# A row-sum kernel: the second load moved from ahead of the opening barriers to behind them

## The chip, the cores and the metric

The kernel runs on one core of a Trainium2 chip. The metric is the device time of one execution, in microseconds (us). Before the change the median of three runs is 160.56 us (160.53 to 160.62).

## The reference

```python
def setup_inputs():
    batch, seq, dim = 32, 512, 1024
    return {"x": np.random.randn(batch, seq, dim).astype(np.float32)}

def reference(x):
    return np.sum(x, axis=-1).astype(np.float32)
```

16384 rows of 1024 float32 values are summed to one value each: 67.1 MB are read, 64 KB are written, and there is one addition for each value read.

## The kernel before, in words

The rows are spread over the 128 partitions of the on-chip memory, 128 rows to each. `BLOCKS = (113, 15)` cuts a partition's 128 rows into two runs, each contiguous in memory. They are loaded in pieces, in this order (the list `loads`, L92 to L100):

- the *lead*: row 0 of every partition, into a buffer of its own (512 KB in all, 4 KB for each partition);
- seven blocks into three rotating buffers `xt0` to `xt2`: six blocks of 16 rows (8 MB, 64 KB for each partition) and one of 15 rows. Each buffer has a semaphore, `slot0` to `slot2`;
- three pieces of 9, 4 and 2 rows (`CUTS`), and the last row in two pieces of 576 and 448 values (`CUT`).

All loads are issued from SyncE's queue (SP, L139). The lead and the first three blocks wait for nothing, since their buffers are empty. Every later load into a rotating buffer first waits until VectorE (DVE) has reduced the block that lay there (L138).

DVE reduces a block with one `tensor_reduce` over 16 rows (L57), after waiting for the block's semaphore. It does the lead first (L105, L106), then the blocks in order. ScalarE (ACT) takes a share of the rows of the last blocks and pieces (L68), and the last row is summed by DVE in two halves (L75). SP stores the results: the two early stores at L145 when most sums are there, the last 16 sums of each partition at L148.

What sets the order around the change is the code at L164 to L183, which edits the finished program. A program of this kind opens with three barriers at which all five engines meet (they carry the lines L197 and L158 in the profile). At each, an engine drains its own queue, reports to GpSimd (POOL), and waits until GpSimd has collected all reports and releases it. The kernel's own instructions stand in a block behind these barriers. The code takes the first `EARLY` load issues out of that block and puts them in front of SP's first drain, ahead of the first barrier. It may do so because these loads wait for nothing. With `EARLY = 2` the lead and block 0 (16 rows, buffer `xt0`, semaphore `slot0`) are issued there; blocks 1 and 2 follow behind the third barrier.

Of the kernel before, what the change touches and what calls it, by code (L numbers as in the profile page):

```python
# [12 lines left out]
ACT_ROWS = 7  # L13
CUT = 576
CUTS = (0, 9, 13, 15)
EARLY = 2


def row_sums(nc, x: bass.AP, out: bass.AP):
# [136 lines left out]
def kernel(tc: tile.TileContext, x: bass.AP, out: bass.AP):  # L156
# [17 lines left out]
    code = list(body.instructions)  # L174
    loads = [i for i in code if i.engine == sp and i.opcode == "DMACopy"][:EARLY]
    for load in loads:
# [36 lines left out]
```

## Time and profile before

One execution was profiled. Its span runs from the first to the last instruction, here from the issue of the lead on SP.

| quantity | value |
|---|---|
| median of three runs | 160.56 us |
| the profiled execution | 160.63 us |
| its span | 159.3 us |
| DVE busy | 121.6 us |
| ACT busy | 17.2 us |
| read from HBM | 67.11 MB, 422 GB/s over the span |
| lead: issue to landing | 3.4 us |
| block 0: issue to landing | 22.3 us |
| the two early stores, the last store: issue to landing | 1.6, 1.4 us |

In the profile's rows, L139 is line 139 of the kernel; "xt<-in_x_dram" names the destination and the source; "x3" counts instructions. A timeline row has the start in us, the length in us, the engine and line, the operation, and in brackets how long the engine sat idle before it and what ended the wait. SPq, POOLq, ACTq and so on are the instruction queues of the engines: issuing, draining and waiting, not computing. A load's packets are the pieces that the 16 DMA engines move one after the other; in this kernel a packet is one partition's share of a load, so a load has 128 of them, 8 for each DMA engine. "Landing" is the time at which all of a load's data and its semaphore counts have arrived.

### The profile page before, as it was taken

The numbers are of one execution on the slowest core, as the hardware profiler recorded it, in microseconds if no ns is written. First come the engines' busy times: TensorE is split into PE (matmuls) and PEld (weight loads), VectorE is DVE, ScalarE is ACT, GpSimd is POOL, SyncE is SP. The second block draws the span as 40 slices with busy tenths as digits, with TensorE's granted clock in tenths as the row PEclk, the third lists the DMA queues.
The fourth block names the chain that finished last, engine by engine and source line by source line (L and its number), as shares of the span: only waits on it lengthen the run. The fifth ranks groups of instructions, "written<-read, shape, count | busy, mean of one in ns | idle before, by whom it ended". The sixth has DMA issues, their size and how long they took to land.

```text
span 159.3 us, 108 instructions
## 1 busy us (share of the span) xinstructions
DVE 121.6 (76%) x17; ACT 17.2 (11%) x31; POOL 0.2 (0%) x4
## 2 busy tenths in 40 slices
DVE  1100029999499995999869996899959999797685
ACT  3000000000000000000000000000000000394694
POOL 0000000000000000000000000000000000000000
DMA  9969979989699699699699797996996999699994
GB/s 395 527 263 527 477 313 527 411 378 527 280 510 527 263 527 527 263 527 510 280 527 444 346 527 313 477 527 263 527 510 278 463 494 494 296 444 444 395 400 143
DMA packets 2304, 67.18 MB, mean 422 GB/s; under 512 B 640, under 2 KB 768, under 8 KB 1024
## 3 DMA queue, kind: packets, MB, share of 16 engines
q1 hardware_dynamic: 2304, 67.18, 98.1%
HBM read 67.11 MB, written 0.07 MB: 422 GB/s over the span
## 4 chain that ended last, share of the span: by engine, by line
DMA 75%; DVE 22%; SPq 1%; issue 0%
DMA xt<-in_x_dram 51%; DMA tail<-in_x_dram 24%; DVE res L57 22%; SPq L139 1%; DVE pairs L75 0%; DVE res L75 0%
## 5 line engine op out<-in xcount | busy, mean ns | idle before, releaser
L57 DVE TENSOR_REDUCE res<-xt 128x16 f32<-128x16384 f32 (+3 forms) x9 | 118.7, 13191 | 32.5 <-DMA xt<-in_x_dram 32.5
L68 ACT ACTIVATE xt<-xt 128x1024 f32<-128x1024 f32 x15 | 15.6, 1043 | 138.1 <-DMA xt<-in_x_dram 138.1
L68 ACT ACTIVATION_READ_ACCUMULATOR xt<-xt 128x1 f32 x15 | 2.8, 187 | 0.0
L57 DVE TENSOR_REDUCE res<-lead 128x1 f32<-128x1024 f32 x1 | 1.2, 1220 | 1.4 <-DMA lead<-in_x_dram 1.4
L103 DVE MEMSET tail<- 128x1 f32 x1 | 0.1, 59 | 2.0 <-PEq L158 2.0
L68 ACT ACT_TABLE_LOAD x1 | 1.3, 1283 | 1.9 <-PEq L158 1.9
L75 DVE CUSTOM_DVE_ANT_0 pairs<-tail 128x288 f32<-128x288 f32 (+1 forms) x2 | 0.9, 426 | 0.1
L75 DVE CUSTOM_DVE_ANT_0 pairs<-xt 128x512 f32<-128x512 f32 x1 | 0.7, 692 | 0.2 <-DMA xt<-in_x_dram 0.2
L75 DVE DVE_READ_ACCUMULATOR2_ANT res<- 128x1 f32 x2 | 0.2, 82 | 0.0
L197 POOL MEMSET const-uint8-127<- 128x1 uint8 x1 | 0.1, 103 | 0.0
L197 POOL MEMSET const-bfloat16-1.0<- 128x1 bf16 x1 | 0.1, 102 | 0.0
L197 POOL MEMSET const-float32-0.0<- 128x1 f32 x1 | 0.1, 98 | 0.2 <-issue 0.2
L197 POOL MEMSET const-float32-1.0<- 128x1 f32 x1 | 0.1, 98 | 0.0
L75 DVE DVE_READ_ACCUMULATOR2_ANT tail<- 128x1 f32 x1 | 0.1, 80 | 0.0
## 6 DMA issues: line engine op xcount, KB each, us to landing
xt<-in_x_dram SPq DMA_DIRECT2D x1, 7680.0 KB, 39.6
xt<-in_x_dram SPq DMA_DIRECT2D x1, 4608.0 KB, 31.2
xt<-in_x_dram SPq DMA_DIRECT2D x1, 2048.0 KB, 35.7
xt<-in_x_dram SPq DMA_DIRECT2D x1, 1024.0 KB, 37.7
lead<-in_x_dram SPq DMA_DIRECT2D x1, 512.0 KB, 3.4
tail<-in_x_dram SPq DMA_DIRECT2D x1, 288.0 KB, 37.9
tail<-in_x_dram SPq DMA_DIRECT2D x1, 224.0 KB, 38.0
xt<-in_x_dram SPq DMA_DIRECT2D x6, 40.8
```

The lines of the kernel that those rows point to most:

```text
L57: nc.vector.tensor_reduce(out=res[:, c : c + n], in_=t[:, j * D : (j + n) * D].rearrange("p (j d) -> p j d", d=D), axis=X, op=ADD,).then_i ...
L68: nc.scalar.activation(out=v, in_=v, func=COPY, accum_out=res[:, c + i : c + i + 1]).then_inc(act, 1)
L75: nc.vector.tensor_tensor_reduce(out=pairs[:, 0 : h - a], in0=t[:, a:h], in1=t[:, h:b], scale=1.0, scalar=0.0, op0=ADD, op1=ADD, accum_out ...
L103: nc.vector.memset(tail[:, CUT + 15 : CUT + 16], 0.0).then_inc(vec, 1)
L139: nc.sync.dma_start(out=dst, in_=src).then_inc(s, 16)
L197: nc = _bacc.Bacc("TRN2", target_bir_lowering=False, num_devices=1)
```

## The change

The constant `EARLY` goes from 2 to 1.

```diff
 CUT = 576
 CUTS = (0, 9, 13, 15)
-EARLY = 2
+EARLY = 1
```

It is used at one place:

```python
    loads = [i for i in code if i.engine == sp and i.opcode == "DMACopy"][:EARLY]
    for load in loads:
        assert not load.sync_info.on_wait
        code.remove(load)
    body.instructions = code
    code = list(entry.instructions)
    at = next(k for k, i in enumerate(code) if i.engine == sp and i.opcode == "Drain")
    code[at:at] = loads
```

Now the lead alone is issued ahead of SP's first drain. Block 0, that is rows 1 to 16 of each partition, stays in the kernel's own block and is issued behind the third barrier, as the first of SP's instructions there, with blocks 1 and 2 right behind it. The data moved, the sizes, the semaphores and the order of the loads on SP's queue stay as they are.

## The prediction

> **What bounds the kernel now.** I read the page's shares first, then the transfers of the opening, the opening barriers, and the end. On the page, the first fence, look at the queue's share and at what ends the chain.
>
> ```profile
> span 159.3 us, 108 instructions
> DVE 121.6 (76%) x17; ACT 17.2 (11%) x31; POOL 0.2 (0%) x4
> q1 hardware_dynamic: 2304, 67.18, 98.1%
> DMA 75%; DVE 22%; SPq 1%; issue 0%
> ```
>
> Packets of the one load queue fill 98.1% of the 16 DMA engines' span, whereas VectorE (DVE) is busy 76% of it. The 22% of DVE in the chain are reductions that free a buffer for a load; they do not hold the stream up, as the timeline shows (start, length, instruction, idle time before it):
>
> ```profile
> 0.43 2.29 SPq L139 DMA_DIRECT2D xt<-in_x_dram  x3
> 1.92 1.28 ACT L68 ACT_TABLE_LOAD   x1 [1.92 <-PEq L158]
> 1.99 0.06 DVE L103 MEMSET tail<- 128x1 f32 x1 [1.99 <-PEq L158]
> 3.45 1.22 DVE L57 TENSOR_REDUCE res<-lead 128x1 f32<-128x1024 f32 x1 [1.40 <-DMA lead<-in_x_dram]
> 22.77 17.22 DVE L57 TENSOR_REDUCE res<-xt 128x16 f32<-128x16384 f32 x1 [18.10 <-DMA xt<-in_x_dram]
> ...
> 42.12 17.22 DVE L57 TENSOR_REDUCE res<-xt 128x16 f32<-128x16384 f32 x1 [2.13 <-DMA xt<-in_x_dram]
> 61.66 17.22 DVE L57 TENSOR_REDUCE res<-xt 128x16 f32<-128x16384 f32 x1 [2.31 <-DMA xt<-in_x_dram]
> ```
>
> A block of 16 rows arrives every 19.3 us and is reduced in 17.22. Buffer 0 is free at 22.77 + 17.22 = 39.99 and its next load is issued at 40.02, when block 1 has 2.1 us and block 2 another 19.5 us still to come: over 21 us of queued work. So the end is set by one quantity, how early the DMA engines begin and whether they ever run dry. The only place where they could is the opening, which the next view cuts into slices of 0.1 us from 0 to 4 us (busy tenths, then GB/s; a packet's bytes all count in the slice in which it starts):
>
> ```profile
> DMA  0000000000998749894797989989999000000000
> GB/s 0 0 0 0 0 0 0 0 0 0 246 246 123 164 164 246 205 328 164 287 369 287 492 369 410 410 328 4178 2745 2007 1966 0 0 0 0 0 0 0 0 0
> ```
>
> The lead row's 128 packets of 4 KB start at 1.0 us. The jump to 4178 in the slice at 2.7 us is the first of the 64 KB packets of the 16-row load; the last of the 16 engines reaches its first one in the slice at 3.0 (3.08 in the packet records). The zeros behind it are engines inside packets of 2.4 us. In those records each engine goes from its lead packets to its long ones within about 0.01 us. So the lead row keeps the engines fed until 2.70 (the earliest engine) to 3.08 (the latest), and until then the next load need not be there.
>
> **What the change moves.** Nothing is added or removed: one DMA issue on SyncE's queue (SP) goes from ahead of the first barrier to behind the third. These rows (instruction, duration in ns, first and last start in us) show what it passes:
>
> ```profile
> L197 SPq DRAIN  x1: 125/125/125, 0.9 to 0.9; - x1
> L197 POOLq DRAIN  x1: 181/181/181, 0.3 to 0.3; - x1
> L197 POOLq EVENT_SEMAPHORE  x2: 17/17/17, 1.1 to 1.1; - x2
> L158 SPq DRAIN  x3: 7/7/7, 1.3 to 1.6; - x3
> L158 SPq EVENT_SEMAPHORE  x2: 17/17/17, 1.5 to 1.8; - x2
> ```
>
> The trace has them to the nanosecond. SP issues the lead at 0 (383 ns) and the 16-row load at 0.433 (425 ns), drains from 0.913 to 1.038, and GpSimd, which collects the arrivals, goes on at 1.063. GpSimd itself had drained by 0.481 and the other engines by 0.32: SP is the late one at the first barrier, and the second issue is why. SP leaves the third barrier at 1.855 and issues the next load at 1.915.
>
> Step 1, the barrier. Without the second issue SP's drain starts at about 0.433. With the same 125 ns it ends at 0.558, 0.48 us earlier than 1.038. The bounds: with the 7 ns of later drains GpSimd's own 0.481 would decide, 0.56 earlier; if the drain ended no earlier than now, 0. I take 0.48, since this drain too stands right behind a DMA issue. Behind the first barrier all steps are fixed, so all three shift together.
>
> Step 2, the issue. The moved load takes the place of the one now issued at 1.915: 1.915 - 0.48 = 1.435 (bounds 1.36 and 1.915). It is thus issued 1.00 us later than before, not the 1.48 that the old place suggests.
>
> Step 3, from issue to first packet. For a load into a busy ring the trace shows it nowhere alone. Below: the last store, issued at 157.85, has its first packet at 158.69, 0.83 later; the two stores ahead of it 0.85 and 0.93; the lead 1.01. Above: this load, issued at 0.433, starts at 2.70, so it was ready within 2.27. I take 1.01, since the lead is the nearest in kind: a load from the same tensor with the same 128 packets. It gives 1.435 + 1.01 = 2.44 for the first engine. The lead's packets reach the 16 engines over some 0.35 us, so the last is ready at about 2.79. Needed: 2.70 to 3.08. The engine whose lead ends last, which sets the end, has some 0.3 us to spare; the earliest might idle 0.1 us in the worst pairing, and is not the one that ends last. Cost: 0. Its cover is the lead row; uncovered, each 0.1 us of late start would move the end by 0.1.
>
> Step 4, the loads behind. Blocks 1 and 2 follow on the SP queue: with the 0.33 to 0.49 us spacing of the issues they go out near 1.82 and 2.30 and are needed at about 22 and 41 us. Cost 0, hidden by 19 us of block 0. No further issue moves on SP; GpSimd's queue holds none.
>
> Step 5, the other engines. ScalarE's table load (1.92) and DVE's memset (1.99) come 0.48 earlier; ScalarE works next at 137.8, DVE waits for the lead until 3.45 and then idles 18.10 us. Value 0. The wait of the first block on DVE stays where it is.
>
> Sum: 0 in the profiled execution, whose 159.30 span and 1.33 around it are 160.63; that lies 0.07 above the median of the runs, 160.56, and I put the forecast on the median: 160.56. With the pace of the long packets (2418 to 2482 ns in this opening) falling a little differently, its own range is 160.40 to 160.75. A measurement here can tell about 0.2%, 0.32 us, from no change.
>
> **The rivals.**
> Slower, the queue runs dry: the moved load takes as long as its upper bound, 2.27, from issue to first packet. Then it starts at 1.435 + 2.27 = 3.71. If every engine is ready then, the end moves by 3.71 - 3.08 = 0.63; if the engines' 0.38 spread is added again, by 1.01: 161.19 to 161.57. It counts as slower from the point where the last engine's first long packet starts after 3.08 + 0.32 = 3.40. For it: the upper bound excludes nothing, and the packets here are 16 times the lead's. Against it: 0.83 to 1.01 in all four issues that can be seen, from 60-byte to 4 KB packets.
> The Trainium skill (DMA: Bandwidth & Descriptors, "Latency and other measured facts") says that an HBM access takes 0.2 us on average and up to 2 us at high load; as an estimate, an issue that ends at 1.435 + 0.33 = 1.76 would then start near 3.76, 0.68 behind the latest engine, which is this rival. No row here shows it: the long packets under full load follow one another without a gap.
>
> Faster, the lead row flows better: its 128 packets took 211 ns on average where undisturbed ones took 159, so 8 on each engine could end 8 x 0.052 = 0.42 us sooner if the second load's preparation disturbed them. The new load would then bind at 2.44 to 2.79, so the end gains 0.29 at the last engine; with the lower 0.83 and the earliest barrier up to the 0.42: 160.14 to 160.27. Against it: the slow packets begin with the first one, before anything else is in the queue.
>
> The barrier doesn't move: SP still arrives late, the load is issued at 1.915 and starts at 2.93 to 3.28, so the last engine loses up to 0.2: 160.56 to 160.76. Against it stands GpSimd's 0.481. That the change does nothing of what it says, with the load kept ahead, would leave 160.56 too; the list of issues that are moved is cut at one, so I give it nothing.
>
> **How the numbers follow.** Covered: 0.57. Queue dry: 0.28, of which 0.25 beyond 0.2% and 0.03 inside it. Lead faster: 0.10, hardly any of it inside. Barrier unmoved: 0.05, as good as no change. Of the covered case 0.03 on each side is left to a pace of the long packets that differs by more than 0.32 in 154 us. So faster 0.13, same 0.59, slower 0.28. The predicted time is that of the likeliest, 160.56. The range runs from 160.22, which leaves out the far half of the faster case, to 161.20, which takes in the dry queue up to its 0.63 and leaves the rest out.
>
> **What would show it.** Step 1: SP's first drain near 0.43, and ScalarE's table load at about 1.44. Step 2: three load issues in a row from about 1.44. Step 3: in slices of 0.1 us, the jump to thousands of GB/s still at 2.7 with no empty slice before it; the first 16-row reduction still at 22.8. A zero slice between lead and jump, or that reduction later than 23.1, proves the forecast wrong to the slow side; a reduction before 22.5, to the fast side. Steps 4 and 5: DVE's idle time ahead of later blocks still 2.1 to 2.3 and ended by the loads.

## The result and the profile after

The changed kernel takes 162.35 us (median of six runs, 162.09 to 163.09) against 160.59 us (160.49 to 160.65) before: ratio 1.0115, 95% interval 1.0101 to 1.013. It is 1.8 us slower, and it also varies more: 1.0 us between its runs instead of 0.16. The profiled execution is the one of 162.09, the fastest of the six, with a span of 160.8 us where before it was 159.3.

The page after: span, the load queue's share, the chain by engine.

```profile
span 160.8 us, 108 instructions
...
q1 hardware_dynamic: 2304, 67.18, 97.5%
...
DMA 75%; DVE 22%; SPq 1%; issue 0%; DVEq 0%
```

The bytes and the packets are the same; the queue's share fell from 98.1 to 97.5%. The transfers still set the end. The timeline after, with the rows that answer to those shown of before:

```profile
1.43 59.88 SPq L139 DMA_DIRECT2D xt<-in_x_dram  x5
1.43 1.28 ACT L68 ACT_TABLE_LOAD   x1 [1.43 <-PEq L158]
1.50 0.06 DVE L103 MEMSET tail<- 128x1 f32 x1 [1.50 <-PEq L158]
3.31 1.22 DVE L57 TENSOR_REDUCE res<-lead 128x1 f32<-128x1024 f32 x1 [1.75 <-DMA lead<-in_x_dram]
24.38 17.22 DVE L57 TENSOR_REDUCE res<-xt 128x16 f32<-128x16384 f32 x1 [19.85 <-DMA xt<-in_x_dram]
43.74 17.22 DVE L57 TENSOR_REDUCE res<-xt 128x16 f32<-128x16384 f32 x1 [2.13 <-DMA xt<-in_x_dram]
63.09 17.22 DVE L57 TENSOR_REDUCE res<-xt 128x16 f32<-128x16384 f32 x1 [2.13 <-DMA xt<-in_x_dram]
```

The lead's reduction starts 0.14 us earlier, the first block's 1.61 later (24.38 against 22.77), and the next ones 1.62 and 1.43 later, with 2.13 us of idle time before each of them. So the loss arises before the first block has landed, and the rest of the kernel passes it on, but for some 0.2 us: the last store is issued 1.46 us later than before (159.31 against 157.85). Where it arises is seen in the transfers of the first 4 us (slices of 0.1 us; busy tenths, then GB/s). One 64 KB packet started in a slice counts as 655 GB/s.

```profile
DMA  0000000002995677769689699693999990909900
GB/s 0 0 0 0 0 0 0 0 0 82 164 369 123 123 205 205 287 246 451 287 369 532 287 410 533 287 819 123 655 1311 2621 1311 1311 0 655 0 655 655 0 0
```

Before, all 16 engines went to their long packets between 2.70 and 3.08 us, within about 0.01 us of the end of their share of the lead. Now the lead's shares end at 2.49 to 2.96. Two engines go straight on, at 2.64 and 2.82; the other 14 stand idle first and start later: ten between 2.94 and 3.26, and then single ones at 3.46, 3.69 and 3.78, each a lone 655 in its slice, and at 4.10, behind this view. The barriers did what was forecast (instruction, duration in ns, first and last start in us):

```profile
L197 POOLq EVENT_SEMAPHORE  x2: 17/17/17, 0.6 to 0.7; - x2
...
L197 SPq DRAIN  x1: 132/132/132, 0.4 to 0.4; - x1
```

SP drains from 0.420 to 0.552, GpSimd goes on at 0.578 (1.063 before), and the load is issued at 1.430.

The two parts of the loss in this execution can be read from the packet records. The last engine starts its first long packet at 4.095 instead of 3.080: 1.02 us. That packet takes 3.03 us instead of 2.42: 0.61. Together 1.63; block 0 lands 1.62 later (24.36 against 22.74). All 16 first packets are long, 2.66 to 3.22 us, while before 14 of the 16 took 2.42 and the slowest 2.48.

### The profile page after: what moved, and what is told of

Same layout as the page of the kernel before. It is cut to its first block, busy times and chain, and to the rows that moved or that the text cites. A ratio compares the mean times of both kernels' runs of the same rounds, so it can differ in the third digit from the quotient of the medians.

```text
span 160.8 us, 108 instructions
## 1 busy us (share of the span) xinstructions
DVE 121.6 (76%) x17; ACT 17.2 (11%) x31; POOL 0.2 (0%) x4
## 3 DMA queue, kind: packets, MB, share of 16 engines
q1 hardware_dynamic: 2304, 67.18, 97.5%
## 4 chain that ended last, share of the span: by engine, by line
DMA 75%; DVE 22%; SPq 1%; issue 0%; DVEq 0%
DMA xt<-in_x_dram 75%; DVE res L57 21%; DVE pairs L75 1%; SPq L139 1%; DVE tail L75 0%; DVE res L75 0%; DVEq L131 0%
```

## The experiments

Each kernel was timed beside the kernel before on the same chip, which there took 160.75 to 160.85 us; the ratio is to those runs. Times of issues and packets are from the start of the span of the one execution that was profiled; the medians are over all runs. An engine "runs dry" when it has moved every packet that has reached it. Diffs are against the changed kernel.

**Cover: a longer lead.** Three rows instead of one, with block 0 behind the barriers (lead3) and ahead of them (lead3_e2, `EARLY = 2`); later two rows (lead2). The blocks have 15 rows to make room, so there is one small block more, in the control too.

```diff
+LEAD = 3
...
-    xt = [sbuf(f"xt{i}", G * D) for i in range(BUFS)]
-    lead = sbuf("lead", D)
+    xt = [sbuf(f"xt{i}", (G - 1) * D) for i in range(BUFS)]
+    lead = sbuf("lead", LEAD * D)
...
-    loads = [(0, lead[:, :], xs[0][:, 0:D], sems["first"])]
+    loads = [(0, lead[:, :], xs[0][:, 0 : LEAD * D], sems["first"])]
...
-    rows_dve(lead, 0, 1, sums[0], 0)
+    rows_dve(lead, 0, LEAD, sums[0], 0)
```

> The lead is three rows long (the blocks behind it 15 rows), block 0 still behind the barriers. Theory D (the queue runs dry: block 0 reaches the engines 1.2 to 2.7 us after its issue, when the one-row lead is over at 2.5 to 3.0, and then restarts cold): the lead now lasts until about 5.2 us, so the long packets start there without a gap and at 2.42 us each from the first; time equal within 0.2% to the same kernel with block 0 ahead of the barriers, some 160.6 us. Rival P (the place behind the barriers itself spoils the stream): still 1.5 to 2 us above that kernel, about 162.3.

> The control for the run with a three-row lead: the same kernel with block 0 ahead of the barriers, as in the kernel before. Both theories: 160.4 to 160.9 us.

Measured: lead3 160.95 us, ratio 1.0006 (0.9996 to 1.0015); lead3_e2 160.88 us, 1.0003 (0.9994 to 1.0013). The loss is gone although the load is issued at the same 1.43 us. The transfers of lead3 from 4 to 8 us:

```profile
DMA  9598599955899299990000000000000000999999
GB/s 492 246 737 369 246 492 492 614 246 246 369 1352 1352 123 3072 1229 2458 1229 0 0 0 0 0 0 0 0 0 0 0 0 0 0 0 0 614 1229 614 2458 1843 2458
```

The lead's packets run on until the long ones (60 KB here, 614 GB/s each) start at 5.16 to 5.79 us. The next ones start from 7.4 us on, 2.27 us later, so every first packet has its full pace. The place behind the barriers costs nothing in itself: theory D holds here, rival P falls.

> The change with a lead of two rows (blocks of 15 rows), which lasts until about 4.0 to 4.4 us. The late engines started at 3.8 to 5.3 us in the runs with one row, so two rows cover most but not all of them: 160.8 to 161.8 us, with no or few engines late. If a lead of any length delayed block 0 by as much again, because its traffic lasts longer: 162 us or more.

Measured: 161.90 us, ratio 1.0071 (1.0052 to 1.009), just above the forecast. The two-row lead lasts until 4.1 to 4.6; the long packets start at 4.10 to 5.15, and all 16 first ones take 2.36 to 3.00 us instead of 2.27. So even a load issued 2.7 us or more ahead of the lead's end was not in time everywhere.

**Neighbours: what else happens at that moment.** Blocks 1 and 2 were held back (gap), the table load was put off (table_late), and both (quiet).

```diff
+        if b == 1:
+            nc.sync.wait_ge(vec, 2)
         nc.sync.dma_start(out=dst, in_=src).then_inc(s, 16)
```

```diff
+    nc.scalar.wait_ge(slots[0], 16)
+    nc.scalar.preload_act_table(COPY)
     nc.vector.memset(tail[:, CUT + 15 : CUT + 16], 0.0).then_inc(vec, 1)
```

> One-row lead, block 0 behind the barriers as in the change, but SP issues blocks 1 and 2 only when the lead row is reduced (about 4.6 us), so that block 0 is alone on the way. Rival C (crowding: the two issues right behind block 0 delay its descriptors): first long packets within 0.4 us of each other, all by about 3.0 us, time 160.6 to 161.2. Theory D: the spread from 2.6 to 4.1 us and the long first packets stay, 162.1 to 163.1.

> The change, with ScalarE's table load put off until block 0 has landed, so that it no longer falls into the time in which block 0 starts. Rival T (the table load disturbs the start): 160.6 to 161.2 us. Theory D and rival C: unchanged, 162.1 to 163.1.

> The change with both other neighbours taken away at once: ScalarE's table load waits until block 0 has landed, and blocks 1 and 2 are issued only when the lead is reduced. If each of the two is enough to delay block 0, so that taking away one alone showed nothing: all engines start block 0 within 0.4 us, by about 3.2, time 160.6 to 161.4 us. Theory M (the lead's own traffic is enough): single engines still start 1 us or more after the others, first packets about 3 us, 162.1 to 163.4 us.

Measured: gap 162.64 us, ratio 1.0114 (1.008 to 1.0148); table_late 162.34, 1.0104 (1.0082 to 1.0126); quiet 162.57, 1.0121 (1.0082 to 1.016). None of the neighbours, alone or together, is the cause. The view of gap from 2 to 6 us shows the late engines most plainly:

```profile
DMA  9989879999900000000090999090990000009990
GB/s 451 410 328 532 369 328 492 410 901 2704 656 0 0 0 0 0 0 0 0 0 1311 0 655 655 655 0 1311 0 655 1311 0 0 0 0 0 0 655 1966 1311 0
```

Six engines pass from the lead to block 0 at 2.86 to 3.09 us. Then no packet starts for 0.9 us, and the other ten follow at 4.01 to 4.97, long after the lead's last packet ended at 3.09: 2.6 to 3.5 us after the issue at 1.43.

**What the engines do when they are idle.** In dry, SP issues block 0 only when the lead has landed. In swap, block 0 is issued first, ahead of the lead (both ahead of the barriers).

```diff
+        if dst.tensor.name == "xt0" and b == 0:
+            nc.sync.wait_ge(sems["first"], 16)
         nc.sync.dma_start(out=dst, in_=src).then_inc(s, 16)
```

```diff
-EARLY = 1
+EARLY = 2
...
+    loads[0], loads[1] = loads[1], loads[0]
     last = xt[n_bufs % BUFS]
```

> The change, with SP issuing block 0 only when the lead row has landed (about 3.4 us), so that all engines are idle and no lead traffic is left. Theory L: first packets spread over 1 us or more from about 4.4 us, some 3 us each; time 163.5 to 165 us. Rival H: first packets within 0.4 us of each other from 4.4 us, 2.42 us each; time about 160.6 + (4.8 - 3.1) = 162.3 us.

> Both loads ahead of the barriers as before, but block 0 (64 KB packets) issued first and the lead row second, so that the large packets find idle engines at the very start, with no lead traffic and no barrier near them. Theory L (large packets that find idle engines start late and spread, and their first ones take long, whatever is around them): first packets from 1.0 us on, spread over 1 us or more, some 3 us each instead of 2.42; time 161.3 to 162.5 us. Rival H (the lead row's traffic delays block 0's start in the changed kernel) and rival R (only a ring that has run dry and is filled again is slow): first packets within 0.4 us, 2.42 us each, time 160.3 to 160.9.

Measured: dry 163.18 us, ratio 1.0147 (1.0132 to 1.0162), between the two forecasts; swap 160.96, 1.0008 (0.9999 to 1.0018), 0.06 above what H and R gave. The view of dry from 2 to 6 us, then swap from 0 to 4:

```profile
DMA  8899799930100000000000009999000009000000
GB/s 369 369 492 451 328 451 451 410 123 0 41 0 0 0 0 0 0 0 0 0 0 0 0 0 1966 3277 2621 1311 0 0 0 0 0 1311 0 0 0 0 0 0
```

```profile
DMA  0000000000999900090000000000000000000000
GB/s 0 0 0 0 0 0 0 0 0 0 3932 2621 1311 1311 0 0 0 1311 0 0 0 0 0 0 0 0 0 0 0 0 0 0 0 0 0 0 0 0 0 0
```

In dry, 14 engines start within 0.22 us of each other, 0.98 to 1.20 after the issue at 3.515, and two at 1.84. In swap, 14 start at 1.01 to 1.37 and two at 1.71 and 1.79. That is tidier than in the changed kernel, so large packets are not late of themselves. But 13 of 16 first packets in dry take 2.99 to 3.63 us, 13 of 16 in swap 3.02 to 3.62, where the second ones take 2.42 to 2.48: that half of theory L holds. On the whole swap is no slower than the kernel before by more than the noise (160.96 against 160.85). A likely reason is that the lead, now behind block 0, no longer pays for the start: in the kernel before its packets took 211 ns on average instead of 159, an estimated 8 x 0.052 = 0.4 us for an engine.

**Packet size.** Block 0 in two loads, one row and then 15.

```diff
+        if b == 0:
+            loads.append((b, xt[0][:, 0:D], xs[k][:, c * D : (c + 1) * D], sems["row1"]))
+            loads.append((b, xt[0][:, D : m * D], xs[k][:, (c + 1) * D : (c + m) * D], slots[0]))
+            continue
```

> The change, with block 0 loaded in two parts behind the barriers: one row (4 KB packets) and right behind it 15 rows (60 KB packets). Theory L: the small packets are there by about 2.5 to 2.8 us, as the lead's were 1.0 to 1.35 after its issue, and they cover the start of the large ones until about 4.1; time 160.6 to 161.2 us. Rival R: the small packets come late as well, from 2.6 to 4.1 us, and the time stays at 162.1 to 163.1.

Measured: 162.26 us, ratio 1.0091 (1.0068 to 1.0113). The row's 4 KB packets begin at 2.87 us, 1.43 after their issue, and some engines have theirs only after 3.7, while the last engine ends the lead at 3.24. So single engines get them late, like the large ones. The 60 KB packets behind them start at 4.51 to 5.79 and 12 of 16 have their full pace of 2.27 at once: the row covered them, but its own delay was the loss. Theory L falls.

**The queue.** The lead goes out from ScalarE's queue.

```diff
-        nc.sync.dma_start(out=dst, in_=src).then_inc(s, 16)
+        eng = nc.scalar if s is sems["first"] else nc.sync
+        eng.dma_start(out=dst, in_=src).then_inc(s, 16)
...
-    at = next(k for k, i in enumerate(code) if i.engine == sp and i.opcode == "Drain")
+    at = next(k for k, i in enumerate(code) if i.engine == act and i.opcode == "Drain")
```

> The change, with the lead issued from ScalarE's queue (ahead of ScalarE's first drain) instead of SP's, so that block 0 meets the same traffic on the same 16 engines but is the first load on its own queue. Theory S (block 0 is late because its packets stand in the same queue as a lead that is still moving): block 0 starts 0.98 to 1.4 us after its issue, beside the lead's packets, nothing runs dry: 160.6 to 161.3 us. Theory M (what delays it is that the engines and the memory are busy with the lead's start, whatever the queue): first long packets 1.2 to 2.7 us after the issue or later, and some 3 us long: 161.8 to 163.1 us.

Measured: 162.65 us, ratio 1.0118 (1.0089 to 1.0146). Block 0, issued at 1.57 as the first load of its queue (the lead at 0.13), starts at 3.01 to 4.37, 1.4 to 2.8 us later. Theory S falls.

**The moment of the issue.** A place behind the first barrier (behind1, and again in more rounds), behind the second (behind2, and with the neighbours taken away: quiet_b2), and a later issue (late).

```diff
+    nxt = next(i for i in body.instructions if i.engine == sp and i.opcode == "DMACopy")
+    body.instructions = [i for i in body.instructions if i is not nxt]
+    seen = 0
+    for blk in fn.blocks:
+        code = list(blk.instructions)
+        for k, i in enumerate(code):
+            if i.engine == sp and i.opcode == "EventSemaphore":
+                seen += 1
+                if seen == 1:
+                    code[k + 1 : k + 1] = [nxt]
...
```

```diff
+    nc.vector.memset(pairs[0][:, :], 0.0).then_inc(vec, 1)
+    count["vec"] += 1
     nc.vector.wait_ge(sems["first"], 16)
...
+        if s is slots[0] and b == 0:
+            nc.sync.wait_ge(vec, 2)
```

> Block 0 is issued right behind the first barrier instead of the third (at about 0.75 us instead of 1.43). Theory D: the engines need 1.2 to 2.7 us from issue to first packet, so they have it at 1.95 to 3.4; the lead covers until 2.5 to 3.0, so most engines go on without a gap and a few start late: 160.6 to 161.3 us. A rival in which any place behind a barrier costs the same: 162.1 to 163.1.

> The kernel with block 0 right behind the first barrier again, in more rounds: does it beat the kernel before? Theory D: both keep the engines fed from the lead to the end, so the same time within 0.1%. It is faster only if the barriers that end earlier count for something: up to 0.2 us.

> Block 0 is issued behind the second barrier, at about 1.1 us, between the place behind the first (0.79, no loss) and behind the third (1.43, 1.6 us lost). Theory M: the lead's first packets start at 1.0, so this issue already meets them: some engines start late and the first packets are up to 3 us long: 161.0 to 162.3 us. If only the order of arrival against the end of the lead counts, with the 1.0 us of an idle engine: 160.6 to 160.9 us.

> Block 0 behind the second barrier (issue at about 1.13), with the same two neighbours taken away. If they were what spoiled the run with block 0 at this place: 160.6 to 161.2 us, every long packet 2.42 us from the first or second on. Theory M: single engines late by 1 to 2 us and packets of about 3 us, 162 to 163.6 us.

> The change, with block 0 issued still later, at about 2.1 us, when VectorE has cleared a buffer of 512 values. Theory M: the lead's traffic is nearly over by then, so the way from issue to first packet is nearer to the 0.98 to 1.8 us of the run with idle engines: first packets at 3.1 to 3.9, 3.1 us long, time 161.9 to 162.8 us, no more than in the changed kernel although the issue is 0.7 us later. If the delay from the issue is the same whatever the traffic, 1.2 to 2.7 us: first packets at 3.3 to 4.8, time 162.7 to 163.8.

| kernel | issue of block 0 | starts of its first packets | those packets | median us | ratio (95%) |
|---|---|---|---|---|---|
| before | 0.43 | 2.70 to 3.08 | 2.42 to 2.48 | 160.59 | |
| behind1 | 0.79 | 2.73 to 3.27 | 2.42 to 2.59 | 160.68 | 0.9992 (0.9982 to 1.0001) |
| behind1_long | 0.78 | 2.75 to 3.18 | 2.42 to 2.44 | 160.66 | 0.9993 (0.9984 to 1.0001) |
| behind2 | 1.13 | 2.66 to 5.33 | 2.42 to 3.41 | 163.23 | 1.0132 (1.0092 to 1.0172) |
| quiet_b2 | 1.12 | 2.61 to 4.90 | 2.42 to 3.04 | 163.10 | 1.0141 (1.0124 to 1.0158) |
| the change | 1.43 | 2.64 to 4.10 | 2.66 to 3.22 | 162.35 | 1.0115 (1.0101 to 1.013) |
| late | 2.16 | 3.12 to 4.87 | 2.42 to 3.51 | 162.88 | 1.0125 (1.0097 to 1.0153) |
| dry | 3.52 | 4.49 to 5.36 | 2.42 to 3.63 | 163.18 | 1.0147 (1.0132 to 1.0162) |

The view of behind1 from 0 to 4 us:

```profile
DMA  0000000000997927146979799699999090000000
GB/s 0 0 0 0 0 0 0 0 0 0 205 205 123 123 41 164 41 123 246 369 328 532 328 451 492 287 532 1679 2089 4711 1966 41 655 0 0 0 0 0 0 0
```

The jump is as steep as before, from 2.7 us on, with the load issued 0.36 us later. The time is in theory D's range, and not even the few late engines that it allowed for are seen. The ratios put behind1 some 0.1 us below the kernel before, but both intervals hold 1. Nor could this run show what earlier barriers are worth: only the first ends earlier. SP's drain behind the moved issue takes the gain back, and GpSimd goes on from the second at 1.384 us (1.391 before).

Behind the second barrier, 0.34 us later still, the loss is as large as anywhere, more than any theory had. The view of behind2 from 2 to 6 us:

```profile
DMA  7988899899999009000009000090000009999009
GB/s 328 369 369 369 369 532 983 369 942 2130 2704 1311 655 0 0 655 0 0 0 0 0 655 0 0 0 0 655 0 0 0 0 0 0 1311 3277 1966 1311 0 0 655
```

Twelve engines start by 3.25, close behind the end of their lead, and four at 3.51, 4.13, 4.70 and 5.33, up to 4.2 us after the issue. Little but the issue of block 0 differs from behind1, since its neighbours stand almost where they do there: blocks 1 and 2 go out at 1.86 and 2.24 us (1.90 and 2.28 in behind1), and the table load starts at 1.87 (1.91). In behind2 the second packets of most engines, too, took 2.84 to 3.06 us; in quiet_b2 they took 2.42 to 2.49. That the neighbours lengthen them is not shown: behind1 has nearly the same ones and second packets of 2.42, and gap, where blocks 1 and 2 are held back, has second packets of up to 3.35. In quiet_b2 one engine still comes at 4.90, and the time is no better.

The late issue decides nothing between its two forecasts: 162.88 is 0.08 above the end of the first one's range, and the four runs are 1.4 us apart. 12 engines start 0.96 to 1.38 after the issue, as idle ones do, and the last four 1.98 to 2.71 after it.

## Why the prediction was wrong

**Steps 1 and 2** held to 0.01 us: the drain 132 ns (125 was assumed), the barriers 0.485 earlier, the issue at 1.430 (forecast 1.435). Steps 4 and 5 held too: blocks 1 and 2 go out at 1.81 and 2.29, later blocks show 2.13 us of idle time, and putting the table load off (table_late) changes nothing.

**Step 3 failed**, "from issue to first packet": "I take 1.01, since the lead is the nearest in kind", and with it "Cost: 0". In the profiled execution the step put block 0 back by 1.63 us: 1.02 for the late start of the last engine and 0.61 for its long first packet. Three things in it were wrong.

- The size. 1.01 is what an idle engine needs: 0.98 to 1.20 for 14 engines in dry. With the lead on the way it was 1.21 to 2.67 us in the changed kernel, up to 3.5 in gap and 4.2 in behind2. None of the four issues that the sum was based on had met a load that was just starting. The lead and the last store found idle engines, and the two early stores found engines that were finishing the last load (its packets ran until 156.93, theirs start at 156.96 and 157.43).
- The upper bound. 2.27 is the time of the earliest engine, for an issue at 0.43; the same rows give 3.08 - 0.43 = 2.65 for the latest, and the changed kernel's 2.67 is just beyond that. But a bound for one issue is none for an issue at another moment: the ten late engines of gap took 2.6 to 3.5 us.
- A term that was missing: the length of the first packets, 2.66 to 3.22 us instead of 2.42. Starting in time was not enough, for the two that followed their lead without a gap took 3.03 and 3.05. What makes a packet long is not shown. In dry and swap only first packets were long, but in gap and behind2 second ones were too, which had been waiting behind the first. The trace before showed the like, in the lead's own first packets of 0.18 to 0.70 us where most later ones took 0.159; the prediction used that row only for the rival of a faster lead.

**The rival "the queue runs dry"** was the right mechanism, and was given 0.28. Its price was 0.63 to 1.01. Its upper end was met almost exactly by the late start, 1.02, which is partly luck: with the same issue the latest engine took 2.67 us here, 2.96 in table_late and 3.54 in gap. The long packet's 0.61 came on top, and the range ended at 161.20 while the profiled execution stands at 162.09 and the median at 162.35. One of the two signs named for it came true, the first reduction after 23.1, at 24.38. The other, an empty slice between the lead and the jump, did not, because the engines went over one by one. The test of it is the longer lead: the same issue at 1.43, the same barriers, no loss.

The Trainium skill's rule on HBM accesses (DMA: Bandwidth & Descriptors, "Latency and other measured facts": 0.2 us on average, up to 2 us at high load) pointed the right way. By it, as an estimate, the load would have started near 3.76; it started at 2.64 to 4.10. That the memory is what delays it is not shown by these runs.

The other rivals: the lead did not run measurably better alone (a mean packet of 200 ns here and 217 to 225 in gap, table_late, quiet and dry; 211 before), and the barriers did move.

**What stays open** is why single engines get the packets of a load 2 to 4 us after its issue when another load is just on its way, and why an issue at 0.79 escapes this while one at 1.13 does not. It is not the size of the packets (split), not the shared queue (lead_act), not the issues behind it or the table load (gap, table_late, quiet). The lead's first packets start at 1.0, between the two; that this is the border is only a guess. Nor does the distance to the lead's end alone decide: 1.9 to 2.5 us sufficed in behind1, while 2.7 to 3.1 did not in lead2.

## What to carry to other kernels

When a transfer-bound kernel opens with a small load, the next load should be issued so early that every DMA engine has it queued before its share of the small one is done; the latency read off idle engines is not the measure. In this kernel an issue 0.43 or 0.79 us after the first was free and one at 1.13 us or later lost 1.4 to 2.5 us. If the second load must be late, the first one must last longer: three rows (until 5.2 to 5.8 us) covered an issue at 1.43, two rows did not.

## What had not been expected of the hardware

A short disturbance at the start lasts to the end. A load's 128 partitions are shared out to the 16 engines, 8 each, so an engine that starts late ends late: the times at which the 16 engines finish block 0 are 1.41 us apart after the change (0.34 before), and 134 us later, at the last load, they are still 1.37 apart (0.40 before). Nothing in this trace evens it out, and the slowest engine sets the time.

A start that is half in time is also uncertain: between the runs of one kernel the time varies by 0.13 to 0.5 us where the engines never run dry (the kernel before, behind1, swap, lead3, lead3_e2), by 1.0 in the changed kernel, 1.4 in quiet and 1.7 in behind2, but by 0.14 again in dry, where all engines are idle when the load comes. The kernels that lose have four runs each, the changed one six, and quiet_b2 with its 0.3 does not fit.

SP's drain behind a load issue took 125 and 132 ns, and its later drains 7. SP was the last to arrive at the first barrier in both kernels; the second load issue ahead of it delayed all five engines by 0.485 us.
